# Layer-1 mixer: an earlier start of the k chain, and 16x16 blocks inverted on GpSimd instead of three levels on TensorE

## The chip, the cores and the metric

The kernel runs on 1 core of one Trainium2 chip. The time is device microseconds of that core, as the median of several executions. TensorE is called PE here, VectorE DVE, ScalarE ACT, GpSimd POOL and SyncE SP, as in the profile.

## What is computed

The reference is a two-layer decoder trunk over 256 tokens of width 1024. Each layer is a mixer, a cross-attention into 256 memory tokens and a gated MLP, each followed by `x <- LayerNorm(alpha * x + sublayer(x))`. The change lies in the mixer of layer 1, a chunked gated DeltaNet with 8 heads of 128 and chunks of 64 tokens. Cut to what matters:

```
q, k, v, z, bl, al = split(x @ w_in)            # 4 x 1024 columns, and 2 x 8
q, k, v = split(silu(causal_dwconv(qkv, conv_w)))
qh, kh = l2norm(q) * 128**-0.5, l2norm(k)
beta = sigmoid(bl);  g = -exp(a_log) * softplus(al + dt_bias);  gc = cumsum(g) within a chunk
decay = exp(gc_t - gc_s) for s <= t, else 0
m = strictly lower part of ((kh * beta) kh^T * decay)     # 64x64 for each head and chunk
tinv = inverse of (eye + m)                              # unit lower triangular
u = tinv @ (v * beta);  w = tinv @ (kh * beta * exp(gc))
qk = (qh kh^T) * decay
for each chunk:  v_new = u - w @ state
                 out = (qh * exp(gc)) @ state + qk @ v_new
                 state = state * exp(gc_last) + (kh * exp(gc_last - gc))^T v_new
o = rms_norm(out) * silu(z);  return o @ w_out
```

## The kernel before

Weights come from DRAM in 1 MB pieces on SP's queue (`load`), are split into a rounded part `wh` (ACT, L151) and a rest `wl` (DVE, L153), and each product is made of three PE passes (`mm3`, L158 to L160, and `mm3n`, L164 to L166). One 128-column piece of a projection is 24 such matmuls, and its result goes through the causal convolution (ACT L926, three DVE taps L929) and a Silu (L934).

The 8 heads are worked in two groups of four, and the tokens in two halves `tt` of 128, that is two chunks each. For a group and a half, `gdn_pre` makes the decay `dT` (from `pg`, PE), k, q and v transposed (`pk`, `pq`, `pv`), the products `pK` and `pQ`, the masked and scaled triangle `LT` and its transpose `L` (from `pL`). The inverse `Z` of (eye + m) is then built by doubling: level 0 is a mask and a difference on DVE, and levels 1 to 6 in `gdn_inv` each take two products on PE (`pA` of Z and a part of L, `pZ` of X and A) and one transpose (`pX`), with copies on ACT (`Lc`, `X`, half of the next Z) and a mask and a difference on DVE. `gdn_rec` runs the recursion over the two halves and normalises the result: `pvn`, `pS` and `pon` on PE, `vn` and `zg` on DVE, and a power on POOL (`rsqrt`, L135) between two DVE steps on `zg` (L1131 and L1135).

The order of PE's instructions is written by hand. `weave` runs a chain, a generator whose `yield n` asks for n steps of another generator, the fill, in between; the numbers come from the table `NW`. A fill step is 6 matmuls of a projection, or 3 of 512 columns. Instructions issued before the first `yield 0`, and those of all other engines, are placed by the scheduler of the framework. Every engine runs its own instructions strictly in order.

Before, the gate projection z of group 0, the k projection, `scalars()` (beta and the decay rates g, through `pl` and `pgc`), and the q and v projections of group 0 stand ahead of the chain. The fill of group 0's chain are the k, q and v projections of group 1 (`group_1`), that of group 1's prologue the z projection, and that of the last recursion the output projection (`res["head"]`).

Of the kernel before, what the change touches and what calls it, by code (L numbers as in the profile page):

```python
# [14 lines left out]
ALU = mybir.AluOpType  # L15
# [11 lines left out]
RMS_EPS = 1e-6  # L27
LAM_INIT = 0.8 - 0.6 * math.exp(-0.3 * 0)
NLEV = 6
NTAIL = 8  # L30
NEARLY = 6
AHEAD = 2
NW = [3, 2.6, 1, 2.5, 1, 1.2, 0.7, 3, 2, 3, 4, 1, 6, 2, 0, 5.2, 0.3, 3]
NEG = -1e30

def _constants():
    s = np.arange(P)[:, None]
    t = np.arange(P)[None, :]
# [50 lines left out]
def hybrid_trunk(ctx: ExitStack, tc: tile.TileContext, a: dict, const: dict, out: bass.AP, dbg=None):  # L89
# [110 lines left out]
    def proj_t(*args):  # L200
        run(proj_t_gen(*args))
# [666 lines left out]
    def mixer_c(h, hT, sm, smq, fill, res):  # L868
# [101 lines left out]
        def bank(name):  # L970
            return mm(name).rearrange("p (g t) -> p g t", t=P)
# [16 lines left out]
        tts = nc.vector.tensor_tensor  # L988

        def level_tile():  # L990
            return smq.tile([P, 4, 64], F32, tag="A", name="A")

        def heads(x):
            return x.unsqueeze(1).broadcast_to([x.shape[0], 4, 64])
# [3 lines left out]
            for g in range(4):  # L998
                nc.scalar.activation(junk[:, g], src[:, g], AF.Square, accum_out=dst[:, g:g + 1])

        def gdn_pre(grp, tt, o):
            tsl = slice(tt * P, tt * P + P)
            cs = slice(tt * 8 + grp * 4, tt * 8 + grp * 4 + 4)
            q, k, v = (qkvT[x, grp][:, :, tsl] for x in "qkv")
            sc = sm.tile([P, 6, 4], F32, tag="sc", name="sc", bufs=4)
# [21 lines left out]
            yield NW[7 + grp]  # L1027
            pq = bank("pq")
            tr4(pq, q)
            sum_sq(sc[:, 1], pq)  # L1030
            pv = bank("pv")
            tr4(pv, v)

            nc.vector.tensor_scalar(sc[:, 0:2], sc[:, 0:2], RMS_EPS, None, op0=ALU.add)
# [3 lines left out]
            nc.vector.tensor_scalar(sc[:, 4], sc[:, 1], RMS_EPS * P, None, op0=ALU.mult)  # L1040
            o["b"], o["eq"] = sc[:, 3], sc[:, 4]
            vx = o["vx"] = keep("vx", grp, tt)
            for g in range(4):
                nc.scalar.mul(vx[:, g], pv[:, g], sc[:, 2, g:g + 1])
            if tt:
                tts(qg, qg, q, op=ALU.mult)
            yield
# [11 lines left out]
            pL = bank("pL")
            tr4(pL, LT)  # L1060
            L = o["L"] = t2("L")
            nc.scalar.copy(L, pL)

            Z = o["Z"] = t2("Z")
            nc.scalar.copy(Z, row(C("ident1")))
            A = level_tile()
            zu = Z.rearrange("p g (u r b) -> p g u r b", u=2, r=2)[:, :, :, 1]
            tts(A, LT.rearrange("p g (n u) -> p g n u", u=2)[..., 1], heads(C("imask")), op=ALU.mult)
            tts(zu, zu, A.rearrange("p g (b u) -> p g u b", u=2), op=ALU.subtract)
            yield  # L1070

        def gdn_inv(o):
            Z, L = o["Z"], o["L"]
            for lev in range(1, NLEV + 1):

                last = lev == NLEV
                half = slice(0, 64)
# [32 lines left out]
                yield NW[9] if "kgx" in o and lev == NLEV else None  # L1110
# [339 lines left out]
```

## Time and profile before

| | |
|---|---|
| median of 3 runs | 943.89 us (941.56 to 945.12) |
| the profiled execution | 942.03 us, span 940.3 us |
| mean granted TensorE clock | 0.992 |
| PE busy | 917.3 us, 98% of the span |
| DVE, ACT, POOL busy | 689.1, 532.6, 36.0 us |
| the stretch of the change | about 503 to 659 us of the span |

The times below are us from the start of the span. In a row of a timeline stand the start, how long, the engine, the line, the operation, the tile written and the tiles read, the shape, the number of instructions merged, and in brackets idle time before it and what ended it. Matmuls overlap, so that the distance of two starts says more than a duration. A 32-bit matmul of the chain shows as two instructions.

### The profile page before, as it was taken

To read this page: it belongs to the slowest core of one execution; us is meant where nothing else is said; L and a number is where in the kernel's file an instruction comes from. 1 tells how busy PE (TensorE), PEld (TensorE's weight loads), DVE (VectorE), ACT (ScalarE), POOL (GpSimd) and SP (SyncE) were. 2 spreads that over 40 slices of the span, in tenths; PEclk is the share of its full clock that TensorE was granted. 3 is DMA by queue.
4 is the path that set the end of the run, shared out by engine and by line. 5 is a ranking of instruction groups with operands and counts; after the bars stand their busy time and mean duration, and the time that the engine had idled before them with its cause. 6 is when DMAs were issued, how large, how long until landed. Compare 5 with 4: busy or idle time off the path is not lost. (4 is left out here: it accounts for less than half of the span.)

```text
span 940.3 us, 15842 instructions
## 1 busy us (share of the span) xinstructions
PE 917.3 (98%) x6284; PEld 820.6 (87%) x6284; DVE 689.1 (73%) x1155; ACT 532.6 (57%) x945; POOL 36.0 (4%) x49
## 2 busy tenths in 40 slices
PE   6999999999999999999999999999999999999996
PEld 5887798889988999998889999888889789999885
DVE  5497586776458999984687975754697889999554
ACT  4753466445444766663357876664364476666440
POOL 1000001000000000000010100000200000000000
PEclk9999999999999999999999999997999999999998
DMA  7843345555573566655566441211444546665541
GB/s 247 293 147 108 117 135 183 177 180 179 190 251 97 180 198 209 209 193 182 179 189 190 136 127 54 91 46 45 151 163 136 177 137 213 207 206 182 189 170 45
DMA packets 101715, 152.89 MB, mean 163 GB/s; under 512 B 5225, under 2 KB 73673, under 8 KB 101641
## 3 DMA queue, kind: packets, MB, share of 16 engines
q1 hardware_dynamic: 99576, 145.08, 46.9%
q0 software_dynamic: 2064, 6.80, 2.2%
q8 instruction: 50, 0.82, 0.4%
q14 instruction: 25, 0.20, 0.1%
HBM read 150.81 MB, written 1.05 MB: 162 GB/s over the span
## 5 line engine op out<-in xcount | busy, mean ns | idle before, releaser
L153 DVE TENSOR_TENSOR wl<-raw,wh 128x1024 fp32r<-128x1024 f32 x268 | 325.4, 1222 | 116.0 <-ACT wh L151 113.3
L151 ACT CAST wh<-raw 128x1024 fp32r<-128x1024 f32 x268 | 278.9, 1052 | 229.3 <-PE ps_f L159 53.1
L158 PE MATMUL ps_f<-hT,wh 128*128 128x256 f32 x576 | 159.0, 276 | 0.0
L159 PE MATMUL ps_f<-hT,wh 128*128 128x256 f32 x576 | 159.0, 276 | 0.0
L160 PE MATMUL ps_f<-hT,wl 128*128 128x256 f32 x576 | 159.0, 276 | 0.0
L158 PEld LDWEIGHTS ps_f<-hT,wh 128*128 128x128 f32 x576 | 108.1, 188 | 0.0
L159 PEld LDWEIGHTS ps_f<-hT,wh 128*128 128x128 f32 x576 | 108.1, 188 | 0.0
L160 PEld LDWEIGHTS ps_f<-hT,wl 128*128 128x128 f32 x576 | 108.1, 188 | 0.0
L158 PE MATMUL ps_t<-hT,wh 128*128 128x256 f32 x352 | 100.5, 286 | 0.0
L159 PE MATMUL ps_t<-hT,wh 128*128 128x256 f32 x352 | 97.9, 278 | 0.0
L160 PE MATMUL ps_t<-hT,wl 128*128 128x256 f32 x352 | 97.8, 278 | 0.0
L164 PE MATMUL ps_o<-wh,aT 128*128 128x512 f32 x176 | 69.2, 393 | 0.0
L165 PE MATMUL ps_o<-wl,aT 128*128 128x512 f32 x176 | 68.8, 391 | 0.0
L166 PE MATMUL ps_o<-wh,aT 128*128 128x512 f32 x176 | 68.6, 390 | 0.0
L158 PEld LDWEIGHTS ps_t<-hT,wh 128*128 128x128 f32 x352 | 66.1, 188 | 0.7
L159 PEld LDWEIGHTS ps_t<-hT,wh 128*128 128x128 f32 x352 | 66.4, 189 | 0.1
L160 PEld LDWEIGHTS ps_t<-hT,wl 128*128 128x128 f32 x352 | 66.3, 188 | 0.0
L302 PE MATMUL ps<-wh,hT 128*128 128x512 f32 x192 | 54.3, 401 | 0.0
L302 PEld LDWEIGHTS ps<-wh,hT 128*128 128x128 f32 x192 | 36.0, 191 | 8.4 <-DVE hT L381 0.5
L1311 ACT ACTIVATE fy<-ps_f,fcw 128x256 f32<-128x256 f32 x72 | 40.2, 559 | 0.0
L164 PEld LDWEIGHTS ps_o<-wh,aT 128*128 128x128 f32 x176 | 33.0, 188 | 7.6 <-issue 0.5
L166 PEld LDWEIGHTS ps_o<-wh,aT 128*128 128x128 f32 x176 | 33.0, 188 | 7.3
(359 smaller groups left out, 1843.0 us busy)
## 6 DMA issues: line engine op xcount, KB each, us to landing
raw<-in_ffn_w_in SPq DMA_DIRECT2D x44, 1024.0 KB, 5.5
raw<-in_w_in SPq DMA_DIRECT2D x26, 1024.0 KB, 5.7
raw<-in_ffn_w_out SPq DMA_DIRECT2D x22, 1024.0 KB, 5.0
raw<-in_xa_wkv SPq DMA_DIRECT2D x16, 1024.0 KB, 5.3
raw<-in_w_mix_out SPq DMA_DIRECT2D x8, 1024.0 KB, 5.1
raw<-in_xa_wq SPq DMA_DIRECT2D x8, 1024.0 KB, 7.9
raw<-in_xa_wo SPq DMA_DIRECT2D x8, 1024.0 KB, 5.0
lngb<-in_ln_g POOLq DMA_DIRECT2D x6, 512.0 KB, 4.5
```

The source lines that it names most:

```text
L151: nc.scalar.copy(hi, src)
L153: nc.vector.tensor_tensor(lo, src, hi.bitcast(F32), op=ALU.subtract)
L158: nc.tensor.matmul(ps, lh, rh, start=first, stop=False)
L159: nc.tensor.matmul(ps, lh, rl, start=False, stop=False)
L160: nc.tensor.matmul(ps, ll, rh, start=False, stop=last)
L164: nc.tensor.matmul(ps, lh, rh, start=first, stop=False)
L165: nc.tensor.matmul(ps, lh, rl, start=False, stop=False)
L166: nc.tensor.matmul(ps, ll, rh, start=False, stop=last)
L302: nc.tensor.matmul(ps, x, ww[:, k], start=k0 + k == 0 and ww is wh and not xl, stop=k0 + k == KT - 1 and ww is wl)
L1311: nc.scalar.activation(yt, ps, AF.Identity, scale=cw[:, 2, mc:mc + 1], bias=cw[:, 3, mc:mc + 1])
```

## The change

- Levels 1 to 3 go, and level 0 with them. `LT` is written to DRAM (L1048), read back as 64 blocks of 16x16, one to a partition (`base_load`, L1086), and each block's inverse is found by substitution on POOL (`base_solve`: one scaling, 14 times a product and a difference, one memset). The result goes to DRAM (L1100) and comes back (`zc`, L1104) to be spread into `Z` by two DVE products (L1113). `gdn_inv` then does levels 4 to 6.
- `gdn_pre` is cut in two: `gdn_pre_k` needs k alone and ends with `L`; `gdn_pre_q` does q, v and `pQ`.
- The chain starts when k is there. The projections q and v of group 0, then k, q, v of group 1, then z, are one line of fill; `until` gives fill until a named projection is made. After group 0's solve is issued come q and v, then `gdn_pre_q`, k of group 1, `gdn_inv`; after group 1's solve come the recursion of group 0, v, `gdn_pre_q` and `gdn_inv` of group 1.

```diff
-NW = [3, 2.6, 1, 2.5, 1, 1.2, 0.7, 3, 2, 3, 4, 1, 6, 2, 0, 5.2, 0.3, 3]
+NW = [3, 2.6, 1, 2, 1, 1.5, 0.7, 1, 1, 8, 4, 1, 6, 2, 0, 5.2, 0.5, 2]
...
-        def gdn_pre(grp, tt, o):
+        def gdn_pre_k(grp, tt, o):
...
+            nc.gpsimd.dma_start(scr_in[grp][tt * 4:tt * 4 + 4, :P * P].rearrange("g (s t) -> s g t", t=P), LT)
+            pL = bank("pL")
+            tr4(pL, LT)
+            L = o["L"] = t2("L")
+            nc.scalar.copy(L, pL)
+            yield
...
+        def base_load(grp):
+            src = scr_in[grp].rearrange("a b -> (a b)").rearrange("(p x) -> p x", x=BASE * (P + 1))
+            src = src[:, :BASE * P].rearrange("p (i t) -> p i t", t=P)[:, :, :BASE]
...
+            nc.gpsimd.dma_start(m, src)
...
+        def base_solve(grp, os_):
+            m, z = blocks[grp]
+            eng = nc.gpsimd
+            eng.tensor_scalar(z, m, -1.0, None, op0=ALU.mult)
+            for i in range(1, BASE - 1):
...
+                eng.tensor_tensor(t, z[:, :i, i:i + 1].broadcast_to(sh), m[:, i:i + 1, i + 1:].broadcast_to(sh), op=ALU.mult)
+                eng.tensor_tensor(z[:, :i, i + 1:], z[:, :i, i + 1:], t, op=ALU.subtract)
+            eng.memset(z.rearrange("p i j -> p (i j)")[:, ::BASE + 1], 1.0)
+            nc.gpsimd.dma_start(scr_out[grp], z.rearrange("p i j -> p (i j)"))
...
+                nc.gpsimd.dma_start(zc, back[tt])
...
-            for lev in range(1, NLEV + 1):
+            for lev in range(4, NLEV + 1):
...
-        proj_t(*proj_c(0, "q"))
-        proj_t(*proj_c(0, "v"))
...
-        fill.gens.append(group_1())
-        yield from steps(NW[3], gdn_pre(0, 0, os_[0][0]), gdn_pre(0, 1, os_[0][1]))
-        yield from steps(NW[4], gdn_inv(os_[0][0]), gdn_inv(os_[0][1]))
-        fill.rest()
-        fill.gens.append(proj_z(1))
-        yield from steps(NW[5], gdn_pre(1, 0, os_[1][0]), gdn_pre(1, 1, os_[1][1]))
+        fill.gens += [fills(), proj_z(1)]
+        yield from units(NW[3], gdn_pre_k, 0)
+        base_load(0)
+        base_solve(0, os_[0])
+        yield from until("v", 0)
+        yield from units(NW[7], gdn_pre_q, 0)
+        yield from until("k", 1)
+        yield from inv(NW[4], 0)
+        yield from until("q", 1)
+        yield from units(NW[5], gdn_pre_k, 1)
+        base_load(1)
+        base_solve(1, os_[1])
         outs = []
-        yield from steps(NW[16], gdn_inv(os_[1][0]), gdn_inv(os_[1][1]), gdn_rec(0, os_[0], outs))
-        fill.rest()
+        yield from steps(NW[8], gdn_rec(0, os_[0], outs))
+        yield from until("v", 1)
+        yield from units(NW[8], gdn_pre_q, 1)
+        yield NW[9]
...
+        yield from inv(NW[16], 1)
```

First place: PE behind the k projection. `pl` transposes the scalars, `pgc` sums the decay rates, `ps_t` is a projection. Before:

```order
L160 MATMUL ps_t_5179<-hT_4502,wl_5116 128x256
L899 MATMUL pl_5209<-c_all_96,linT_5044 128x16 x4
L158 MATMUL ps_t_5252<-hT_4501,wh_5238 128x256
L159 MATMUL ps_t_5252<-hT_4503,wh_5238 128x256
L160 MATMUL ps_t_5252<-hT_4501,wl_5239 128x256
```

Now:

```order
L160 MATMUL ps_t_5185<-hT_4502,wl_5122 128x256
L899 MATMUL pl_5215<-c_all_96,linT_5050 128x16 x4
L917 MATMUL pgc_5232<-gg_4964,c_m1_4955 128x16 x2
L990 MATMUL pg_5244<-c_m1_4955,gg_4964 128x128 x4
L986 MATMUL pk_5249<-c_all_96,ck_5074 128x128 x4
L990 MATMUL pg_5268<-c_m1_4955,gg_4964 128x128 x4
L986 MATMUL pk_5273<-c_all_96,ck_5074 128x128 x4
L158 MATMUL ps_t_5308<-hT_4501,wh_5294 128x256
```

49 fill matmuls stood between `pl` and `pgc` before, and 143 more ahead of the first `pg`; now none does.

Second place: POOL around the norms of group 0's recursion (`sc_6444`, `sc_6489` now; `sc_6694`, `sc_6771` before). Before:

```order
L1037 TENSOR_TENSOR sc<-sc,phalf 128x4 x4
L135 TENSOR_TENSOR sc_6694<-sc_6694,mhalf 128x4
L135 TENSOR_TENSOR sc_6771<-sc_6771,mhalf 128x4
L135 TENSOR_TENSOR sc_7048<-sc_7048,mhalf 128x4
L393 DMA lngb<-in_ln_g 128x1024
L135 TENSOR_TENSOR sc_7103<-sc_7103,mhalf 128x4
```

Now, with the end of group 1's solve:

```order
L1098 TENSOR_TENSOR base<-base,bt 64x11x4
L1097 TENSOR_TENSOR bt<-base 64x36
L135 TENSOR_TENSOR sc_6444<-sc_6444,mhalf 128x4
L1098 TENSOR_TENSOR base<-base,bt 64x12x3
L1097 TENSOR_TENSOR bt<-base 64x26
L1098 TENSOR_TENSOR base<-base,bt 64x13x2
L1097 TENSOR_TENSOR bt<-base 64x14
L1098 TENSOR_TENSOR base<-base,bt 64x14
L1100 DMA scr_out<-base 64x256
L1104 DMA zc<-scr_out 128x4x16 x2
L135 TENSOR_TENSOR sc_6489<-sc_6489,mhalf 128x4
```

The first norm's power stands behind 25 of the solve's 30 instructions, and the second behind all of it, the store of the result and the issue of its two loads.

Third place: DVE in the recursion of group 0, between the two values `vn`. Before:

```order
L1131 TENSOR_TENSOR zg<-pon,h 128x512
L1133 SCALAR_TENSOR_TENSOR sc_6694<-sc_6694,sc 128x4
L1089 TENSOR_TENSOR A<-pA,c_m_4955 64x256
L1135 TENSOR_TENSOR zg<-zg,sc_6694 128x512
L1124 TENSOR_TENSOR vn<-pvn,sc 128x512
L1108 TENSOR_TENSOR Z<-Z,pZ 128x8x32 x2
L1131 TENSOR_TENSOR zg<-pon,h 128x512
L1133 SCALAR_TENSOR_TENSOR sc_6771<-sc_6771,sc 128x4
```

Now:

```order
L1166 TENSOR_TENSOR vn<-pvn,sc 128x512
L1173 TENSOR_TENSOR zg<-pon,h 128x512
L1175 SCALAR_TENSOR_TENSOR sc_6444<-sc_6444,sc 128x4
L929 SCALAR_TENSOR_TENSOR cv<-ps_t,gcw,cv 128x253
L1177 TENSOR_TENSOR zg<-zg,sc_6444 128x512
L929 SCALAR_TENSOR_TENSOR cv<-ps_t,gcw,cv 128x254
L1166 TENSOR_TENSOR vn<-pvn,sc 128x512
L929 SCALAR_TENSOR_TENSOR cv<-ps_t,gcw,cv 128x255
L153 TENSOR_TENSOR wl<-raw,wh 128x1024
L1173 TENSOR_TENSOR zg<-pon,h 128x512
```

The multiplication of `zg` by the power (L1177, before L1135) still stands ahead of the second `vn`; behind it now stand taps of the convolution and weight splits instead of the steps of the levels.

## Rows read from the trace of the kernel before

**Rows 1.** The page, busy time of each engine, share of the span, instructions.

```profile
PE 917.3 (98%) x6284; PEld 820.6 (87%) x6284; DVE 689.1 (73%) x1155; ACT 532.6 (57%) x945; POOL 36.0 (4%) x49
```

**Rows 2.** Timeline of PE in the mixer, the rows after a wait of its own.

```profile
541.29 1.16 PE L986 MATMUL pK<-ck 128*128 128x128 f32 x8 [1.20 <-ACT vx L1044]
...
603.60 0.66 PE L982 MATMUL pq<-c_all,cq 128*128 128x128 f32 x4 [1.04 <-ACT kq L1019]
...
615.47 0.68 PE L986 MATMUL pA<-Z,Lc 128*64 128x64 f32 x8 [0.75 <-ACT Lc L1081]
...
636.39 1.97 PE L986 MATMUL pZ<-A,X 64*128 64x64 f32 x16 [0.59 <-ACT Z L1101]
```

**Rows 3.** Windows: length, busy of PE, PEld, DVE, ACT, POOL, granted clock, DMA, GB/s.

```profile
648.40:658.80 10.40, 9.84 (x61) 9.19 (x60) 3.54 (x7) 2.70 (x5) 0.00 (x0) 0.52 0.16 61
```

**Rows 4.** Timeline of PE, one level of group 0 (start us, us, instruction, count).

```profile
551.10 0.68 PE L986 MATMUL pA<-Z,Lc 128*64 128x64 f32 x8
...
552.88 0.63 PE L1092 MATMUL pX<-c_all,Z 128*64 128x128 f32 x4
553.26 0.37 PE L158 MATMUL ps_t<-hT,wh 128*128 128x256 f32 x1
...
554.60 0.28 PE L160 MATMUL ps_t<-hT,wl 128*128 128x256 f32 x1
554.81 2.00 PE L986 MATMUL pZ<-A,X 64*128 64x64 f32 x16
556.73 0.38 PE L158 MATMUL ps_t<-hT,wh 128*128 128x256 f32 x1
```

**Rows 5.** Timelines of PE and ACT, from the scalars to the first Silu of k.

```profile
501.99 1.06 PE L899 MATMUL pl<-c_all,linT 32*128 32x16 f32 x8
...
505.91 1.05 ACT L151 CAST wh<-raw 128x1024 fp32r<-128x1024 f32 x1 [0.66 <-PE ps_t L159]
506.98 1.28 ACT L907 ACT_TABLE_LOAD   x1
...
509.01 0.59 PE L917 MATMUL pgc<-gg,c_m 128*128 128x16 f32 x4 [0.19 <-issue]
...
509.88 1.28 ACT L920 ACT_TABLE_LOAD   x1
...
511.38 1.28 ACT L934 ACT_TABLE_LOAD   x1
512.67 1.34 ACT L934 ACTIVATE ck<-cv 128x256 f32<-128x256 f32 x4
```

**Rows 6.** Groups by line of DVE: a weight split, and one convolution tap.

```profile
L153 DVE TENSOR_TENSOR wl<-raw,wh 128x1024 fp32r<-128x1024 f32 x268 | 325.4, 1222 | 116.0 <-ACT wh L151 113.3 <-PE pl L899 0.2
...
L929 DVE SCALAR_TENSOR_TENSOR cv<-ps_t,gcw,cv 128x253 f32<-128x253 f32 x24 | 11.3, 475 | 6.6 <-ACT cv L926 6.4
```

**Rows 7.** Timeline of PE, after the first wait of the program.

```profile
10.28 1.97 PE L377 MATMUL pt<-c_all,h 128*128 128x128 f32 x8 [3.67 <-DMA h<-in_x]
11.90 2.31 PE L302 MATMUL ps<-wh,hT 128*128 128x512 f32 x6
...
14.52 1.54 PE L302 MATMUL ps<-wh,hT 128*128 128x512 f32 x6
```

**Rows 8.** Groups by line of POOL: count, busy us, mean ns, idle before.

```profile
L135 POOL TENSOR_TENSOR sc<-sc,mhalf 128x4 f32<-128x4 f32 x4 | 4.1, 1014 | 58.1 <-DVE sc L1133 53.8 <-ACT wh L151 4.4
L1037 POOL TENSOR_TENSOR sc<-sc,phalf 128x4 f32<-128x4 f32 x4 | 4.9, 1228 | 122.5 <-DVE sc L1036 122.5
L1435 POOL MEMSET const-float32-1.0<- 128x1 f32 x1 | 0.1, 100 | 0.0
```

**Rows 9.** DMA issues: count, KB each, median us from issue to landing.

```profile
out<-h SPq DMA_DIRECT2D x4, 256.0 KB, 2.0
...
raw<-in_w_in SPq DMA_DIRECT2D x2, 64.0 KB, 6.1
...
ng<-in_gdn_norm POOLq DMA_DIRECT2D x1, 0.5 KB, 2.3
```

More of the change, by code (lines that the diff above doesn't have):

```diff
@@ L29 @@
 NLEV = 6
+BASE = 16
 NTAIL = 8
@@ L64, in _constants @@
     add("m1", "sums", np.concatenate([s <= t, s > t], axis=1))
-    add("m1", "imask", masks[0][:, halves[0]])
-    add("m1", "cmasks", np.concatenate([s % (64 >> lev) == t[:, :64] % (64 >> lev) for lev in range(1, NLEV)], axis=1))
-    add("m1", "ident1", s == t // 64 * 2 + t % 32 * 4 + t % 64 // 32)
+    add("m1", "blocks", s[:, :1] // BASE == np.arange(P // BASE)[None, :] % 4 * 2 + np.arange(P // BASE)[None, :] // 4)
+    add("m1", "cmasks", np.concatenate([s % (64 >> lev) == t[:, :64] % (64 >> lev) for lev in range(4, NLEV)], axis=1))
     add("m1", "dmask", np.where(s <= t, 0.0, NEG))
@@ L958, in t2 @@
             return smq.tile(B4, F32, tag="t2", name=name, bufs=8)
+        scr = ctx.enter_context(tc.tile_pool(name="scr", bufs=2, space=bass.MemoryType.DRAM))
+        scr_in = [scr.tile([8, P * (P + 1)], F32, name="scr_in") for _ in range(2)]
+        scr_out = [scr.tile([8 * P // BASE, BASE * BASE], F32, name="scr_out") for _ in range(2)]
         held = {}
@@ L990, in level_tile @@
         def level_tile():
-            return smq.tile([P, 4, 64], F32, tag="A", name="A")
+            return smq.tile([P, 4, 64], F32, tag="A", name="A", bufs=2)
         def heads(x):
@@ L999, in sum_sq @@
                 nc.scalar.activation(junk[:, g], src[:, g], AF.Square, accum_out=dst[:, g:g + 1])
-        def gdn_pre(grp, tt, o):
+        def gdn_pre_k(grp, tt, o):
             tsl = slice(tt * P, tt * P + P)
             cs = slice(tt * 8 + grp * 4, tt * 8 + grp * 4 + 4)
-            q, k, v = (qkvT[x, grp][:, :, tsl] for x in "qkv")
-            sc = sm.tile([P, 6, 4], F32, tag="sc", name="sc", bufs=4)
+            k = qkvT["k", grp][:, :, tsl]
+            sc = o["sc"] = sm.tile([P, 6, 4], F32, tag="sc", name="sc", bufs=4)
             pg = bank("pg")
@@ L1026, in gdn_pre @@
                 tts(kg, pk, col(egs[:, 1, cs]), op=ALU.mult)
[L1027 to L1036, printed above, removed]
+            yield
+            nc.vector.tensor_scalar(sc[:, 0], sc[:, 0], RMS_EPS, None, op0=ALU.add)
             nc.gpsimd.tensor_tensor(sc[:, 2], sc[:, 0], phalf, op=ALU.pow)
@@ L1039, in gdn_pre @@
             nc.vector.tensor_tensor(sc[:, 3], sc[:, 3], beta[:, tt, grp * 4:grp * 4 + 4], op=ALU.mult)
-            nc.vector.tensor_scalar(sc[:, 4], sc[:, 1], RMS_EPS * P, None, op0=ALU.mult)
             o["b"], o["eq"] = sc[:, 3], sc[:, 4]
[L1042 to L1047, printed above, removed]
             pK = bank("pK")
@@ L1053, in gdn_pre, with gdn_pre_q @@
                                                op0=ALU.mult, op1=ALU.mult)
+            yield
+            nc.gpsimd.dma_start(scr_in[grp][tt * 4:tt * 4 + 4, :P * P].rearrange("g (s t) -> s g t", t=P), LT)
[3 more added lines that the diff above has]
+            nc.scalar.copy(L, pL)
+            yield
+        def gdn_pre_q(grp, tt, o):
+            tsl = slice(tt * P, tt * P + P)
+            q, k, v = (qkvT[x, grp][:, :, tsl] for x in "qkv")
+            sc, dT = o["sc"], o["att"]
+            pq = bank("pq")
+            tr4(pq, q)
+            sum_sq(sc[:, 1], pq)
+            pv = bank("pv")
+            tr4(pv, v)
+            nc.vector.tensor_scalar(sc[:, 4], sc[:, 1], RMS_EPS, RMS_EPS * P, op0=ALU.add, op1=ALU.mult)
+            vx = o["vx"] = keep("vx", grp, tt)
+            for g in range(4):
+                nc.scalar.mul(vx[:, g], pv[:, g], sc[:, 2, g:g + 1])
+            if tt:
+                tts(o["qg"], o["qg"], q, op=ALU.mult)
+            yield
             pQ = bank("pQ")
@@ L1057, in gdn_pre @@
             yield
[L1059 to L1062, printed above, removed]
-            Z = o["Z"] = t2("Z")
[L1065 to L1069, printed above, removed]
@@ L1070, in gdn_pre @@
-            yield
-        def gdn_inv(o):
-            Z, L = o["Z"], o["L"]
-            for lev in range(1, NLEV + 1):
+        nb = 8 * P // BASE
+        blocks = {}
+        def base_load(grp):
+            src = scr_in[grp].rearrange("a b -> (a b)").rearrange("(p x) -> p x", x=BASE * (P + 1))
+            src = src[:, :BASE * P].rearrange("p (i t) -> p i t", t=P)[:, :, :BASE]
+            m, z = lnp.tile([P, 512], F32, tag="tok", name="base")[:nb].rearrange("p (a i j) -> a p i j", a=2, j=BASE)
+            nc.gpsimd.dma_start(m, src)
+            blocks[grp] = m, z
@@ new lines, in base_solve @@
+        def base_solve(grp, os_):
[3 more added lines that the diff above has]
+            for i in range(1, BASE - 1):
+                sh = [nb, i, BASE - 1 - i]
+                t = sm.tile([nb, 64], F32, tag="bt", name="bt")[:, :sh[1] * sh[2]].rearrange("p (i j) -> p i j", i=i)
+                eng.tensor_tensor(t, z[:, :i, i:i + 1].broadcast_to(sh), m[:, i:i + 1, i + 1:].broadcast_to(sh), op=ALU.mult)
+                eng.tensor_tensor(z[:, :i, i + 1:], z[:, :i, i + 1:], t, op=ALU.subtract)
+            eng.memset(z.rearrange("p i j -> p (i j)")[:, ::BASE + 1], 1.0)
+            nc.gpsimd.dma_start(scr_out[grp], z.rearrange("p i j -> p (i j)"))
+            back = scr_out[grp].rearrange("(t g b) (i j) -> t (b i) g j", t=2, g=4, j=BASE)
+            for tt in range(2):
+                zc = os_[tt]["zc"] = sm.tile([P, 4, BASE], F32, tag="zc", name="zc")
+                nc.gpsimd.dma_start(zc, back[tt])
@@ L1076, in gdn_inv @@
+        def gdn_inv(o):
+            zc, L = o["zc"], o["L"]
+            Z = o["Z"] = t2("Z")
+            for u in range(2):
+                sh = [P, 4, BASE, 4]
+                tts(Z[:, :, 64 * u:64 * u + 64].rearrange("p g (r b) -> p g r b", b=4),
+                    zc.unsqueeze(3).broadcast_to(sh),
+                    C("blocks")[:, 4 * u:4 * u + 4].unsqueeze(1).unsqueeze(1).broadcast_to(sh), op=ALU.mult)
+            for lev in range(4, NLEV + 1):
                 last = lev == NLEV
@@ L1088, in gdn_inv @@
                 else:
-                    tts(A, pA, heads(cmasks[half, lev - 1]), op=ALU.mult)
+                    tts(A, pA, heads(cmasks[half, lev - 4]), op=ALU.mult)
                 pX = bank("pX")[half, :, cols]
@@ L1109, in gdn_inv @@
                     Z = o["Z"] = Z2
-                yield NW[9] if "kgx" in o and lev == NLEV else None
+                yield
             if "kgx" in o:
@@ L1184, in mixer_c, with fills, until, units @@
             finish()
-        proj_t(*proj_c(0, "q"))
-        proj_t(*proj_c(0, "v"))
-        def group_1():
-            for nm in "kqv":
-                yield from proj_t_gen(*proj_c(1, nm))
-        yield 0
-        fill.gens.append(group_1())
-        yield from steps(NW[3], gdn_pre(0, 0, os_[0][0]), gdn_pre(0, 1, os_[0][1]))
-        yield from steps(NW[4], gdn_inv(os_[0][0]), gdn_inv(os_[0][1]))
-        fill.rest()
-        fill.gens.append(proj_z(1))
-        yield from steps(NW[5], gdn_pre(1, 0, os_[1][0]), gdn_pre(1, 1, os_[1][1]))
+        made = set()
+        def fills():
+            for grp in range(2):
+                for nm in "kqv"[1 - grp:]:
+                    yield from proj_t_gen(*proj_c(grp, nm))
+                    made.add((nm, grp))
+        def until(nm, grp):
+            while (nm, grp) not in made:
+                yield 1
+        def units(n, gen, grp, *args):
+            return steps(n, *(gen(grp, tt, os_[grp][tt]) for tt in range(2)))
+        def inv(n, grp):
+            return steps(n, *(gdn_inv(os_[grp][tt]) for tt in range(2)))
+        yield 0
+        fill.gens += [fills(), proj_z(1)]
[10 more added lines that the diff above has]
+        base_solve(1, os_[1])
         outs = []
-        yield from steps(NW[16], gdn_inv(os_[1][0]), gdn_inv(os_[1][1]), gdn_rec(0, os_[0], outs))
-        fill.rest()
+        yield from steps(NW[8], gdn_rec(0, os_[0], outs))
+        yield from until("v", 1)
+        yield from units(NW[8], gdn_pre_q, 1)
+        yield NW[9]
         new = new_t("oT")
```

## The prediction

> **What bounds the kernel now.** I read the page's busy line first, then the timeline of TensorE (PE) through the layer-1 mixer, then the windows of that stretch, then the rows that price what is new. PE is busy 98% of the span [rows 1], and the mixer holds no long gap: between 503 and 659 us I find single waits of 0.59 to 1.20 us [rows 2]. So whatever PE stops doing shortens the kernel, and whatever makes PE wait lengthens it, microsecond for microsecond. VectorE, ScalarE and GpSimd count only where PE ends up waiting for them. Beside the waits there is one slow stretch: from 648.4 to 658.8 us the granted clock is 0.52 [rows 3], which is the 1.2 GHz level of 1.2 and 2.4, after some 17 us of small matmuls with little fill between.
>
> **The change, part by part.** All is summed against the profiled execution, 942.03 us (span 940.3); the median of the three runs, 943.89, lies 1.9 above it.
>
> *Three levels leave PE.* One level for both token halves is pA, pX, pA, pX, from 551.10 to 553.26, and two pZ, from 554.81 to 556.73 [rows 4]: 2.16 + 1.92 = 4.08 us. Three levels in two groups are 6 x 4.08 = 24.5 us. Each cut between fill and chain also costs about 0.1 us (the last of twelve fill matmuls starts at 554.60, one pitch is 0.12, pZ starts at 554.81 [rows 4]); six cuts fewer net, with the extra pieces of the split prologue, are 0.8. Together **-25.3 us**. VectorE and ScalarE lose their shares of the levels too; PE hid them, so that is worth nothing.
>
> *Old waits go.* The four waits [rows 2] sum to 3.6 us and the places they stand at are rearranged: **-3.6**. The slow clock ran in group 1's levels with almost no fill. That section is now half as long and has one line of fill in it, so I take the 10.4 x 0.48, less the 0.56 us of wait inside it, as gone: **-4.5**.
>
> *The chain begins too early for its scalars.* Before, 49 fill matmuls stand between pl and pgc, and 143 between pgc and pg; now pl, pgc, pg, pk follow each other (the first of the three places of the written order). What PE waits for is in [rows 5]. pl ends at 503.05; the exponent on ScalarE ends at 505.25 (0.66 before the cast at 505.91). Without that cast a table load of 1.28 starts there, and from the end of that load to pgc it took 0.75 (508.26 to 509.01): pgc starts at 507.3, and PE waits 4.2 us. From the end of pgc there are ngc, a table load (1.28), egs, a table load (1.28) and the first Silu, 3.4 us, of which pg hides 0.9; the four Silus (1.34 together) then pace pk by another 0.6. That is 4.2 + 2.5 + 0.6 = **+7.3 us**. No other work covers it: PE runs in its written order and the k projection has ended.
>
> *Smaller new waits.* The second LT now comes behind ScalarE's squares, a table load and a VectorE cast; by the size of the same pair's waits before (1.20 and 1.04 [rows 2]) I take 2 us at pL. pv now stands straight behind the last matmuls of v, whose tile still needs three taps of 0.475 [rows 6], a scaling and a Silu: 1.5. Group 1's recursion loses a piece of fill: 1.5. Together **+5**.
>
> *Restart of the clock.* After 3.67 us of idle at the start of the program six 512-column matmuls took 2.31 us and soon after six took 1.54 [rows 7]. A wait of 5 to 8 us should cost 1 to 2 us in that way: **+1.9** for the first.
>
> *The new side chain.* LT goes to DRAM, comes back as 16x16 blocks, is solved by 30 GpSimd instructions that each wait for the one before, and goes out and in once more. No row shows a plain product or difference on GpSimd. Below stands the memset, 0.10 us; above stand the powers on the same kind of tile, 1.01 and 1.23 us [rows 8]. By form the new instructions are nearest to the power, by work to the memset, with some 14 to 56 columns instead of 1; I take 0.3, three memsets, and keep 0.1 to 1.23 for the range. For the transfers I have a 256 KB store of 2.0 us, a 64-byte-row load of 64 KB with 6.1 us, and 2.3 for the smallest [rows 9]: I take 3 for LT out, 5 for the blocks in, 2.8 for the result out, 3.5 for it back. The whole is 3 + 5 + 30 x 0.3 + 2.8 + 3.5 = 23.3 us from the second LT (from 12 to 55 at the ends).
>
> Group 0: VectorE meets Z<-zc where PE has done pL, 150 fill matmuls (18 us at the pitch of 0.12) and pq, and the last tap has come: about 21 us. It stops for some 2.3; two weight pieces already split (48 matmuls, 5.8 us) less VectorE's own backlog give PE about 4 us. So nothing reaches PE: **0**, up to 34.
>
> Group 1 is worse, and the order shows why (second and third place). The rsqrt of the recursion's first norm stands in GpSimd's queue behind 25 of the 30 instructions, and VectorE, which runs in order, stops at zg until it is there; vn, the taps and the weight splits queue behind zg. Counted from the end of pK: LT 3.6, transfers 8, 25 x 0.3, rsqrt 1.0, then zg, a tap and vn 1.9, so PE could go on at 22, and without the queue it would be there at 15: **+7**. The second rsqrt stands behind the last five, the store's landing and two issues: 1.5 + 2.9 + 1.2 + 1.0, then VectorE's zg, split, taps and the Silu, 3.7, against PE at pv 6.3 after the first: **+4**. One more restart: **+1.9**.
>
> **Sum:** 942.0 - 25.3 - 3.6 - 4.5 + 7.3 + 5 + 1.9 + 0 + 7 + 4 + 1.9 = **935.7** for an execution like the profiled one, 0.7% faster. Against the median I would say 1.9 more, and I settle between: 937. Without any GpSimd wait it is 922.8; each 0.1 us on one GpSimd instruction adds 3 us (25 and 5 in group 1), and 6 once group 0 stops hiding, from about 0.36.
>
> A page speaks against this step. In rows, a weight split on VectorE takes 1.22 us [rows 6] and reads two SBUF tiles; three of them fall into each solve. The Trainium skill, "SBUF — State Buffer", section "Who interferes with whom", says that a VectorE instruction with two SBUF inputs and a GpSimd instruction that reads SBUF exclude each other for the whole instruction. No row here shows the two together. The Trainium skill, "GPSIMD Engine Reference", section "3.1 Elementwise — side-by-side cycle accounting", gives 2.6 cycles an element and a 1.2 GHz engine; by it 56 elements are 0.12 us, and with little else in an instruction the sum would be near 931, an estimate.
>
> **The rivals.**
>
> *All hidden.* With transfers at their shortest and instructions of 0.1 us group 1's rsqrt comes before PE wants it: 923. For it: the memset row. Against it: no row of a reading instruction on GpSimd is below 1 us.
>
> *Shared port.* Three splits of 1.22 lengthen the solve by 3.7 us in group 0, of which 2 reach PE, and about 2.4 in group 1: 936 + 5 = 941. For it: splits are the most common VectorE work [rows 6]; against it: VectorE itself stands still for much of group 1's solve. This is the mechanism of the first page named above.
>
> *GpSimd too slow.* The mechanism of the sum with one other number. At 0.7 us an instruction group 0 costs 9 us and a restart, group 1 17 and 6: 922.8 + 32 + 4 = 959, slower by 1.6%. It decides from about 0.43 us, where the total is back at 942. For it: the powers at 1.01 and 1.23 [rows 8]; against it: their arithmetic.
>
> That the change does not do what it says is excluded: the written order shows the levels gone and the chain begun.
>
> **How the numbers follow.** A measurement of this kernel tells about 0.5% from no change, 4.7 us. Forecast 0.43, mostly 928 to 940; all hidden 0.13; shared port 0.16; too slow 0.28. Faster: 0.13 + nine tenths of 0.43, 0.52. Same: the port case, the edge of the forecast and a little of the slow one, 0.22. Slower: 0.26. The range from 921 to 959 leaves out a tenth at each end.
>
> **What would show it.** Right: twelve fewer pairs of pA and pX rows and no clock of 0.5 between the last levels; PE idle 4 to 5 us before pgc and 2 to 4 before pk, ended by ScalarE; VectorE idle at L1177 ended by GpSimd; L1097 and L1098 near 0.3 us from start to start. Wrong: a pitch above 0.45 there, VectorE waiting more than 5 us at the first L1113 for zc, or PE not waiting at pgc at all.

## Result and profile after: 1.2% slower

The changed kernel takes 953.93 us (median of 4, 953.29 to 954.76) against 942.95 for the kernel before in the same comparison: ratio 1.0115, 95% interval 1.0091 to 1.0139. The forecast was 937 us, faster than before. The profiled execution has a span of 952.7 us, 12.4 more than before.

These are the busy line of the page of the changed kernel, called after here (to be held beside [rows 1]), and the span and mean granted clock of its core:

```profile
PE 903.3 (95%) x6044; PEld 806.0 (85%) x6044; DVE 681.6 (72%) x1131; ACT 518.6 (54%) x907; POOL 66.4 (7%) x121
core 0: 952.7 us, clock 0.976
```

PE is busy 14.0 us less, yet idle 26.4 us more (49.4 against 23.0): together the 12.4. The mean clock fell from 0.992 to 0.976. Both losses lie in the mixer. These are PE's timeline rows there that have idle time before them, in brackets with what ended it; three rows of 0.53 to 0.88 us at the end of the mixer and one of 0.47 are left out:

```profile
506.00 1.00 PE L917 MATMUL pgc<-gg,c_m 128*128 128x16 f32 x4 [4.25 <-issue]
510.51 1.39 PE L986 MATMUL pk<-c_all,ck 128*128 128x128 f32 x4 [1.61 <-ACT ck L934]
...
541.41 0.33 PE L986 MATMUL pv<-c_all,cv 128*128 128x128 f32 x1 [0.53 <-ACT cv L934]
544.05 0.33 PE L986 MATMUL pv<-c_all,cv 128*128 128x128 f32 x1 [2.31 <-ACT cv L934]
...
565.02 0.73 PE L990 MATMUL pA<-Z,Lc 128*64 128x64 f32 x8 [4.31 <-DVE Z L1113]
...
621.56 2.08 PE L990 MATMUL pon<-vn,dT 128*128 128x128 f32 x8 [11.05 <-DVE vn L1166]
...
631.50 0.33 PE L986 MATMUL pv<-c_all,cv 128*128 128x128 f32 x1 [2.76 <-ACT cv L934]
...
646.88 0.67 PE L990 MATMUL pA<-Z,Lc 128*64 128x64 f32 x8 [2.08 <-DVE Z L1113]
```

All waits of the mixer sum to 31.4 us, where before had 4.3 by the same rows (some of them in [rows 2]). Of the seven waits of more than 1 us six are followed by a stretch at the 1.2 GHz level (clock 0.50, or between 0.5 and 1 where a window is slow in part); the exception is the 2.76 us at pv. Windows of after (length, busy PE, PEld, DVE, ACT, POOL, granted clock, DMA, GB/s), to be held against [rows 3]:

```profile
505.00:510.00 5.00, 2.90 (x12) 2.63 (x12) 1.34 (x6) 3.40 (x6) 0.00 (x0) 0.50 0.56 190
510.00:515.00 5.00, 4.49 (x23) 4.12 (x24) 1.26 (x5) 4.41 (x16) 0.00 (x0) 0.57 0.00 0
545.00:550.00 5.00, 5.00 (x33) 5.00 (x32) 0.00 (x0) 2.67 (x15) 2.76 (x6) 0.66 0.49 152
565.00:570.00 5.00, 4.98 (x32) 4.65 (x33) 0.42 (x1) 1.46 (x4) 0.00 (x0) 0.66 0.46 174
620.00:625.00 5.00, 3.44 (x16) 3.44 (x17) 3.18 (x6) 1.56 (x9) 2.76 (x7) 0.50 0.07 15
650.00:655.00 5.00, 5.00 (x20) 4.13 (x21) 1.44 (x3) 1.30 (x3) 0.00 (x0) 0.50 0.00 0
```

What the clock costs I estimate as busy time of PE times one minus the granted clock, over windows of 1 us: 14.5 us in the mixer of after (3.3 at 506 to 515, 1.7 at 545, 1.7 at 565, 2.7 at 621, 5.1 at 647 to 658), 4.8 before. One check on the estimate: the work from the last wait for Z to the first pz takes 30.6 us here and 26.1 in e9 below, where the clock stays at 1.00, so that 4.5 us stand against the 5.1. So the sum is 27.1 us more waits, 9.7 more slow clock, and 23.7 less work (14.0 + 9.7); that makes 13.1, 0.7 more than the 12.4 of the spans; the 0.7 lie in the rest of the program.

The side chain, first GpSimd's own rows in group 0:

```profile
531.18 0.87 POOL L1093 TENSOR_SCALAR base<-base 64x256 f32<-64x256 f32 x1 [4.09 <-DMA base<-scr_in]
532.13 0.20 POOL L1097 TENSOR_TENSOR bt<-base 64x14 f32<-64x14 f32 x1
...
532.42 0.20 POOL L1098 TENSOR_TENSOR base<-base,bt 64x14 f32<-64x14 f32 x1
532.70 1.12 POOL L1097 TENSOR_TENSOR bt<-base 64x26 f32<-64x26 f32 x1
533.90 0.23 POOL L1098 TENSOR_TENSOR base<-base,bt 64x26 f32<-64x26 f32 x1
...
535.58 1.31 POOL L1098 TENSOR_TENSOR base<-base,bt 64x44 f32<-64x44 f32 x1
536.97 0.28 POOL L1097 TENSOR_TENSOR bt<-base 64x50 f32<-64x50 f32 x1
...
546.02 0.62 POOL L1100 DMA_DIRECT2D scr_out<-base  x1 [0.29 <-POOL base L1098]
548.31 1.57 POOL L1104 DMA_DIRECT2D zc<-scr_out  x2 [1.67 <-DMA scr_out<-base]
```

and VectorE's in the same time:

```profile
532.52 1.22 DVE L153 TENSOR_TENSOR wl<-raw,wh 128x1024 fp32r<-128x1024 f32 x1
...
535.55 1.22 DVE L153 TENSOR_TENSOR wl<-raw,wh 128x1024 fp32r<-128x1024 f32 x1
536.68 1.51 DVE L929 SCALAR_TENSOR_TENSOR cv<-ps_t,gcw,cv 128x253 f32<-128x253 f32 x3
...
551.87 0.76 DVE L1113 TENSOR_TENSOR Z<-zc,c_m 128x256 f32<-128x256 f32 x2 [8.39 <-DMA zc<-scr_out]
```

A plain GpSimd instruction takes 0.20 to 0.30 us and follows the one before at 0.3 to 0.36. Five of group 0's take 0.63 to 1.38 instead: each overlaps a VectorE product or difference of two SBUF tiles and ends 0.1 us after it (533.82 against 533.74 for the first, 532.70 + 1.12 and 532.52 + 1.22). Beside the taps, which read PSUM, it is 0.28. The five lose 4.3 us, and the solve takes 14.6 us, 0.49 an instruction. From the second LT (522.8) to zc (551.9) it is 29 us, and VectorE stands for 8.39.

Group 1, GpSimd and then VectorE:

```profile
618.50 0.24 POOL L1097 TENSOR_TENSOR bt<-base 64x36 f32<-64x36 f32 x1
618.70 1.03 POOL L135 TENSOR_TENSOR sc<-sc,mhalf 128x4 f32<-128x4 f32 x1
619.72 0.25 POOL L1098 TENSOR_TENSOR base<-base,bt 64x36 f32<-64x36 f32 x1
```

```profile
619.77 0.75 DVE L1177 TENSOR_TENSOR zg<-zg,sc 128x512 f32<-128x512 f32 x1 [10.08 <-POOL sc L135]
620.44 0.47 DVE L929 SCALAR_TENSOR_TENSOR cv<-ps_t,gcw,cv 128x254 f32<-128x254 f32 x1
620.83 0.67 DVE L1166 TENSOR_TENSOR vn<-pvn,sc 128x512 f32<-128x512 f32 x1
```

The rsqrt runs between two instructions of the solve, zg waits 10.08 us for it, vn stands behind zg, and PE's last pon of group 0 waits 11.05 for vn.

### The profile page after: what moved, and what is told of

It is laid out like the page before. It is cut to its first block, busy times and chain, and to the rows that moved or that the text cites. A ratio compares the mean times of both kernels' runs of the same rounds, so it can differ in the third digit from the quotient of the medians.

```text
span 952.7 us, 15344 instructions
## 1 busy us (share of the span) xinstructions
PE 903.3 (95%) x6044; PEld 806.0 (85%) x6044; DVE 681.6 (72%) x1131; ACT 518.6 (54%) x907; POOL 66.4 (7%) x121
## 5 line engine op out<-in xcount | busy, mean ns | idle before, releaser
L158 PE MATMUL ps_t<-hT,wh 128*128 128x256 f32 x352 | 102.7, 292 | 0.0
L159 PE MATMUL ps_t<-hT,wh 128*128 128x256 f32 x352 | 99.5, 283 | 0.0
L158 PEld LDWEIGHTS ps_t<-hT,wh 128*128 128x128 f32 x352 | 68.5, 194 | 0.5
L159 PEld LDWEIGHTS ps_t<-hT,wh 128*128 128x128 f32 x352 | 68.4, 194 | 0.1
L135 POOL TENSOR_TENSOR lnmv<-lnmv,mhalf 128x1 f32<-128x1 f32 x12 | 11.4, 947 | 479.3 <-DVE lnmv L408 479.3
L164 PEld LDWEIGHTS ps_o<-wh,aT 128*128 128x128 f32 x176 | 33.0, 188 | 7.6 <-issue 0.5
```

The source lines that it names most:

```text
L135: nc.gpsimd.tensor_tensor(dst, src, mhalf[:, :n], op=ALU.pow)
L158: nc.tensor.matmul(ps, lh, rh, start=first, stop=False)
L159: nc.tensor.matmul(ps, lh, rl, start=False, stop=False)
L164: nc.tensor.matmul(ps, lh, rh, start=first, stop=False)
```

## The experiments

Two theories. *Cover*: the levels are worth their 25 us, but the new order leaves too little work between a producer and PE in several places, VectorE's in-order queue carries each delay to PE, and PE pays twice, idle and at 1.2 GHz. *Price*: the solve on GpSimd costs what it saves, wherever it stands. Ratios are to the kernel before in the same comparison, and gains below go by the difference of ratios (0.1% is 0.94 us) unless medians are named.

| run | median us | ratio | interval |
|---|---|---|---|
| change | 953.93 | 1.0115 | 1.0091 to 1.0139 |
| e1 | 946.07 | 1.0036 | 1.0013 to 1.0060 |
| e2 | 946.26 | 1.0054 | 1.0035 to 1.0073 |
| e3 | 950.68 | 1.0105 | 1.0071 to 1.0139 |
| e4 | 962.58 | 1.0209 | 1.0179 to 1.0239 |
| e5 | 955.27 | 1.0157 | 1.0135 to 1.0179 |
| e6 | 958.07 | 1.0187 | 1.0156 to 1.0217 |
| e7 | 938.78 | 0.9981 | 0.9963 to 0.9999 |
| e8 | 939.57 | 1.0000 | 0.9978 to 1.0022 |
| e9 | 945.32 | 1.0038 | 1.0019 to 1.0057 |
| e10 | 946.93 | 1.0052 | 1.0033 to 1.0071 |
| e11 | 919.28 | 0.9761 | 0.9738 to 0.9783 |
| e12 | 959.60 | 1.0186 | 1.0163 to 1.0210 |

**e1, the rsqrt off GpSimd's queue.**

```diff
-                rsqrt(sc[:, 2], sc[:, 1], 4)
+                if grp:
+                    rsqrt(sc[:, 2], sc[:, 1], 4)
+                else:
+                    nc.scalar.activation(sc[:, 2], sc[:, 1], AF.Sqrt)
+                    nc.vector.reciprocal(sc[:, 2], sc[:, 2])
```

> The changed kernel, but the rsqrt of group 0's recursion is a square root on ScalarE and a reciprocal on VectorE, so that it no longer stands in GpSimd's queue behind the solve of group 1. Queue theory (that place in the queue is the cause in group 1): the 11.05 us wait of PE before pon falls under 2 us, and the slow clock after it goes as well, 938 to 941 us. Latency theory (the transfers and the solve together are longer than the work that covers them): VectorE comes to the first Z<-zc of group 1 some 8 to 12 us before zc has landed and stops there in its place, PE waits 6 to 8 us a little later, and the time is 946 to 951 us.

The 11.05 us wait is gone and 7.4 us are won. The median lies at the lower edge of the latency theory's range, well above the queue theory's, and VectorE's rows in e1 show that theory's mark, the stop again one step later:

```profile
633.09 0.76 DVE L1113 TENSOR_TENSOR Z<-zc,c_m 128x256 f32<-128x256 f32 x2 [8.95 <-DMA zc<-scr_out]
```

PE then waits 5.04 us at pv, a little less than expected. The queue was a cause, and the late zc behind it the next one.

**e2, no solve steps.**

```diff
-            for i in range(1, BASE - 1):
+            for i in range(1, 1):
```

> The changed kernel without the 28 product and difference instructions of each solve (the inverse that comes out is not the reference's); the scaling, the memset and all transfers stay. If GpSimd's instructions are what makes the side chain too long: zc of group 0 lands some 13 us earlier, VectorE's 8.4 us stop at the first Z<-zc and PE's 4.3 us wait go, the 11 us wait goes, and the time is 934 to 941 us. If the transfers are what makes it too long (some 14 us in each group), the waits stay at more than half their length and the time is 946 us or more. The waits of PE before pgc and pk (4.25 and 1.6 us) stay in both.

By the number it is the second branch, by the rows neither: VectorE no longer stops in group 0, so the transfers aren't too long there, but of PE's 4.31 us 2.69 stay. In group 1 the rsqrt, which now stood behind the zc issues, still came late, since the load of the blocks alone took 7.8 us from its issue: 7.54 us at zg, 10.6 us of waits at pv. Even without solve steps the change is 0.5% slower than before. So the price of GpSimd's instructions alone is not the cause.

**e3, PE kept busy in two waits.**

```diff
+            if not grp:
+                spin(90)
             mm4(pon, lambda g: o1["att"][:, g], lambda g: vn[:, g], start=False)
...
+            spin(34)
             pg = mm("pgc")
```

> The changed kernel with useless matmuls of fill size in two of PE's waits, 34 before pgc and 90 before the last pon of group 0; nothing reads their result. The waits themselves are as long as before, only PE is not idle in them. Clock theory (each wait is paid a second time, because PE comes out of it at 1.2 GHz): the granted clock is 1.0 from 621 to 630 us and higher from 506 to 515, and the time is 948 to 951 us. Rival (the slow clock belongs to the chain's small 32-bit matmuls, not to the waits): clock and time stay as they are, 953 to 955 us.

The 90 matmuls fill 610.49 to 621.45, and the window behind them, as well as the one behind pgc, now reads 1.00:

```profile
505.00:510.00 5.00, 2.54 (x21) 2.18 (x19) 1.48 (x6) 3.80 (x8) 0.00 (x0) 1.00 0.55 184
...
620.00:625.00 5.00, 5.00 (x43) 4.83 (x42) 1.63 (x3) 2.08 (x10) 2.45 (x4) 1.00 0.15 26
```

That is the clock theory's mark. The median, 950.68, lies in its range too, but that the time moved is not shown: six executions lie between 948.15 and 958.12, and the interval takes in the change's own ratio. The run is also harder on PE than I meant it to be. VectorE had finished vn at 619.35 (the load of the blocks took 4.2 us, not 6.3), so that the 90 matmuls held PE 1.9 us too long, and pk then waits 2.51 us for 1.61, pv 3.43 for 2.76.

**e4, the order alone, levels back on PE.**

```diff
-            for lev in range(4, NLEV + 1):
+            Z, L = o["Z"], o["L"]
+            for lev in range(1, NLEV + 1):
...
-        base_load(0)
-        base_solve(0, os_[0])
```

(with level 0 and its constants as before, and the same for group 1.)

> The changed kernel's order of work (chain begun after k, one line of fill) with the inverse as it was before: levels 0 to 3 on VectorE and TensorE, no scratch transfers, no solve on GpSimd. It shows what the order alone does. If the early start is harmful by itself (waits of 5.9 us before pgc and pk, 2 to 3 at pv, and the slow clock behind them): 949 to 957 us, slower than the kernel before. If the order is harmless and all loss is the side chain's: 941 to 945 us. The waits for vn and for Z in group 0 and the slow clock behind these should be gone in both.

More than either: 19.7 us slower than before, 16.4 us of waits and 10.0 of slow clock in the mixer. It isn't the order in a pure form, since six levels use more of the fill and leave its end bare. But it says which part is harmful: against e4 the change is 9 us faster, so the solve, with all its stalls, is the part that gains.

**e5, the start covered.**

```diff
+        yield 6
         run(extra)
         for finish in late:
             finish()
...
+        yield 4
         yield from units(NW[3], gdn_pre_k, 0)
```

(for this the fill is set up earlier, and Silus of the fill are held back together with k's.)

> The changed kernel with 6 fill steps (36 matmuls, 4.3 us) taken between pl and pgc and 4 (2.8 us) between pgc and the first pg; the Silus of k follow pgc as before. Start theory (the chain begins before its scalars are there, and PE pays for it twice, idle and at 1.2 GHz): the waits of 4.25 and 1.6 us and the slow clock from 506 to 515 us go, some 9 us. Trade theory (these 60 matmuls are missing afterwards as cover of group 0's solve): VectorE's stop at the first Z<-zc grows from 8.4 to some 15 us, PE's wait for Z from 4.3 to 9 to 11 us, and the whole is 950 to 954 us, no gain. If the two don't hang together: 943 to 946 us.

As the trade theory has it, at a smaller size: the start falls from 5.86 to 1.66 us, PE's wait for Z grows to 6.30 with 1.24 more at a fill matmul before it, VectorE's stop grows to 11.88 where I had 15, and pL waits 2.28. Nothing is won; at 955.27 it is even a little worse than I said.

**e6, the same on e4.**

```diff
+        yield 6
         run(extra)
...
+        yield 4
         yield from units(NW[3], gdn_pre_k, 0)
```

> The order of work alone (run e4: inverse on TensorE as before, 962.6 us, 19.7 above the kernel before by the ratio) with the same 6 and 4 fill steps at the start. No solve here needs cover. If the start is the larger part of what the order costs: 950 to 955 us, 8 to 12 less than e4. If the order costs elsewhere (pv right behind v, pL, the norms of group 1 at the end): 957 us or more.

2.1 us less than e4 by the ratios, 4.5 by the medians, with intervals that overlap. As far as four executions of each tell, the start is a smaller part of the order's cost than its own rows say; by e6's rows the rest is pv, pL and the late levels.

**e7, both solves early.**

```diff
+            for nm, grp in (("k", 1), ("q", 0), ("v", 0), ("q", 1), ("v", 1)):
...
+        yield from until("k", 1)
+        yield 2
+        yield from units(1, gdn_pre_k, 1)
+        base_load(1)
+        base_solve(1, os_[1])
         yield from until("v", 0)
```

(with e5's start, one fill step instead of 2 and 1.5 between the pieces of the two `gdn_pre_k`, another pool for group 1's L, four buffers for `zc`, and the same lines taken out further down.)

> Fill in the order k1, q0, v0, q1, v1, z1, so that the k part of both groups comes first and both solves run on GpSimd while q and v of group 0 and group 0's inverse are on TensorE; the start covered by 6 and 4 fill steps; group 1's L in another pool. Latency theory (the levels are worth 25 us, and the side chain of some 29 us only has to be covered by the work that is there): no stop of VectorE at the first Z<-zc, no wait for the rsqrt, slow clock only in group 1's last levels: 917 to 926 us, faster than both kernels. Rival (the solve on GpSimd costs what it saves wherever it stands, through the shared port and the queues): 936 us or more.

My 917 to 926 was wrong; 938.78 lies in the rival's range, but not for its reason: VectorE no longer stops at the first Z<-zc and PE's wait behind the rsqrt is gone, but 22 us of short waits are left (pL 6.4, pv 5.5, pA 4.8 among them).

**e8, e7 with longer solves.**

```diff
-                eng.tensor_tensor(t, z[:, :i, i:i + 1].broadcast_to(sh), m[:, i:i + 1, i + 1:].broadcast_to(sh), op=ALU.mult)
+                for _ in range(2):
+                    eng.tensor_tensor(t, z[:, :i, i:i + 1].broadcast_to(sh), m[:, i:i + 1, i + 1:].broadcast_to(sh), op=ALU.mult)
```

> Run e7 with every product instruction of the solves issued twice, 14 more instructions of 0.2 to 0.3 us in each group, some 5 us each. If the solves are hidden in e7: within 3 us of e7. If GpSimd sets the time: 5 to 10 us more.

0.8 us more by the medians (1.8 by the ratios, with intervals that overlap) for 14 more instructions in each group. By GpSimd's rows the two solves, up to the issue of the store, take 18.3 and 16.8 us where e7 had 11.6 and 12.4, and VectorE still stops at no Z<-zc. The solves are hidden there, and the price theory falls.

**e9, Z of both halves at once.**

```diff
         def inv(n, grp):
+            for tt in range(2):
+                gdn_base(os_[grp][tt])
```

(`gdn_base` is the part of `gdn_inv` with the two products.)

> The changed kernel, but the products that spread zc into Z are issued for both token halves before the first level, so that on VectorE the second half's no longer stand behind taps and weight splits of the fill. If PE's wait for the second Z is VectorE's order of work (2.69 us of it remained in e2, with no solve steps): the waits of 4.31 us in group 0 and 2.08 us in group 1 fall to under 2 and 0.5 us, and 946 to 950 us; 943 if the slow clock behind the second goes too. If it is the late zc alone: no change, 952 to 955 us.

7.3 us won. VectorE still stops for 8.84 us at the first of these products, yet of PE's two waits for Z, 4.31 us has become 1.06 (at pZ) and 2.08 has become 0.34, and there is no slow clock behind either:

```profile
554.22 1.43 DVE L1111 TENSOR_TENSOR Z<-zc,c_m 128x256 f32<-128x256 f32 x4 [8.84 <-DMA zc<-scr_out]
```

```profile
566.60 1.97 PE L990 MATMUL pZ<-A,X 64*128 64x64 f32 x16 [1.06 <-DVE A L1132]
```

In the change the second half's product stood behind taps and a split, as VectorE's rows there show:

```profile
560.07 1.51 DVE L929 SCALAR_TENSOR_TENSOR cv<-ps_t,gcw,cv 128x253 f32<-128x253 f32 x3
561.50 1.21 DVE L153 TENSOR_TENSOR wl<-raw,wh 128x1024 fp32r<-128x1024 f32 x1
...
564.47 0.41 DVE L1113 TENSOR_TENSOR Z<-zc,c_m 128x256 f32<-128x256 f32 x1
```

**e10, fill before pv.**

```diff
         yield from until("v", 0)
+        yield 4
```

(and the same for group 1.)

> The changed kernel with 4 fill steps (24 matmuls, 2.8 us) between the last matmuls of a v projection and pq and pv, in both groups; they are taken from the steps that follow anyway. The waits before pv (0.53 and 2.31 us in group 0 with 1.7 us of slow clock behind, 2.76 us in group 1) go: 946 to 950 us. If VectorE's stop at Z<-zc then only comes out as a longer wait for Z: 951 to 955 us.

5.9 us won, at the lower end of the first expectation. Of the waits at pv 0.25 us stay. Z waits 1.4 us longer, so part was passed on. The last pon of group 0 waits 1.4 longer too, but the edit need not be the cause: the load of group 1's blocks took 7.6 us there, 1.4 more than in the change.

**e11, everything covered.** e7 with the edits of e9 and e10, and

```diff
-        yield 6
+        yield 9
...
-        yield from units(1, gdn_pre_k, 0)
+        yield from units(2, gdn_pre_k, 0)
...
-        yield from units(1, gdn_pre_k, 1)
+        yield from units(2, gdn_pre_k, 1)
```

> Run e7 (both solves early, 938.8 us) with its remaining waits covered by fill steps taken earlier: 9 before pgc, 2 in place of 1 per piece in the k part of both groups, 4 before pq and pv, and the products into Z of both halves at once. e7 had 22 us of PE waits and 6.3 us of slow clock in the mixer. If these short waits are what is left of the change's cost: 918 to 928 us, faster than both kernels. If covering one only opens the next (the fill is used up by the last levels): 932 to 939 us.

919.28 us, 2.4% faster than the kernel before, as expected. Its span is 918.6 us, its mean clock 0.994, and its busy line:

```profile
PE 893.3 (97%) x6044; PEld 798.1 (87%) x6044; DVE 680.9 (74%) x1131; ACT 516.8 (56%) x907; POOL 66.3 (7%) x121
```

The waits of the mixer are 8.2 us and its slow clock 3.2. Which of these edits gave how much was not separated.

**e12, that order with the levels on PE.** e11 with e4's edit in the inverse, and

```diff
-        yield from inv(NW[4], 0)
+        yield from inv(0.5 * NW[4], 0)
...
-        yield from inv(NW[16], 1)
+        yield from inv(0.5 * NW[16], 1)
```

> The order of work and the fill of run e11 (919.3 us), with the inverse as it was before: levels 0 to 3 on VectorE and TensorE, no scratch transfers, no solve; half as much fill for each of the twice as many steps of the levels. If the solve on GpSimd is worth its three levels (25.3 us) once it is covered: 942 to 950 us. If e11 gains by its order instead and the solve adds little: 920 to 935 us.

40 us slower than e11, far over the 942 to 950 of the first theory: PE is busy 33.4 us longer (926.7), 6.5 of it slow clock, and waits 6.3 longer, of which 4.91 are one wait at the transposes (pt) behind the mixer's LayerNorm. So the order alone gains nothing here either; with these fill steps it pays only together with the solve.

## Why the prediction was wrong

The sum, term by term; the measured value is wait plus slow clock behind it, in the profiled execution.

| term | predicted | measured |
|---|---|---|
| levels, cuts | -25.3 | -23.7 |
| old waits | -3.6 | -4.3 |
| start of the chain, restart | +9.2 | +9.2 |
| pL | +2 | 0 |
| pv of group 0 | +1.5 | +4.5 |
| recursion | +1.5 | +0.5 |
| group 0's solve | 0 | +6.0 |
| group 1, first rsqrt, restart | +8.9 | +13.7 |
| group 1, second rsqrt (PE at pv) | +4 | +2.8 |
| last levels: old slow clock gone | -4.5 | +2.4 |
| norms and LayerNorm at the end | 0 | +2.0 |

- **Right:** the mechanism of group 1, the place of the start and its first wait (4.25 us against 4.2), the transfers of group 0 (3.4, 4.9, 2.3, 3.5 against 3, 5, 2.8, 3.5), VectorE's arrival at the first Z<-zc (21 us after the second LT). **Luck:** that the start sums to 9.2 in both columns; pk waited 1.61 us for 3.1, and the slow clock cost 3.3 for 1.9. The measured time lies inside 921 to 959 by luck too: the upper end stood for slow GpSimd instructions.
- **First failed step:** "The slow clock ran in group 1's levels with almost no fill. [...] so I take [it] as gone." It came back: within 1 us of the end of PE's 2.08 us wait for the second Z the clock is at the 1.2 GHz level, and it stays there for 10 us. With that wait gone, e9 shows no such stretch. 6.9 us off; how long the stretch lasts is not settled by the wait, since behind the same wait e2 and e3 lose only 1.6 and 1.5 us.
- **Second:** "So nothing reaches PE: 0". The solve took 14.6 us where the sum had 9: 1.3 of it is the pitch, 4.3 the port. VectorE stopped 8.4 us instead of 2.3; a wait of more than 5 us there was one of my signs of being wrong. The 4.31 us at PE look like that stop less my 4 us of cover, but that is a coincidence: PE's fill runs without a gap to 559.5, long after the stop, e2 and e7 show waits of 2.69 without any such stop, and e9 leaves 1.06 with a stop of 8.84. The wait hung on VectorE's order: I had costed the first half's product and never asked where the second half's stands. 6.0 us off.
- **Third:** the wait behind the rsqrt, 11.05 for 7: from the last LT to the issue of the base load it took 3.9 us where I had 3, the load 6.3 where I had 5, and 25 instructions 8.6 where I had 7.5. The load's share shows in the four traces that have this wait: loads of 4.2, 6.3, 7.6 and 7.8 us (e5, after, e10, e9) go with waits of 8.91, 11.05, 12.41 and 12.59. Slow clock 2.7 for 1.9. 4.8 us off.
- **Fourth:** pv, where three taps, scaling and Silu cost 2.8 us instead of 1.5 and a slow stretch that I had not counted. 3 us off.

Read against e4 instead of the rows, the order is the larger miss. The terms that belong to the order alone (old waits, old slow clock, start, smaller waits) come to +6.1 us in the sum; e4 took 19.7, though its six levels also use more of the fill. The terms of the solve (levels, group 0, both rsqrts) come to -12.4; from e4 to the change it is -9.

The rival "GpSimd too slow" had the sign, not the price: it took 0.7 us an instruction, and they took 0.49 in group 0 (with the port) and 0.35 in the 25 of group 1, so its 959 is not what happened. An instruction of 56 elements beside which no such VectorE instruction ran took 0.28 to 0.30 us, not the 0.12 of the prediction's estimate near 931. The shared port is real, and in group 0 it costs the solve 4.3 us where I had 3.7; of the wait at PE the whole stop explains at most 1.6 us (4.31 less the 2.69 of e2). The Trainium skill, "SBUF — State Buffer", section "Who interferes with whom", says that the two exclude each other; the trace agrees, with the five long instructions of 0.63 to 1.38 us. And of the restarts of the clock I priced two, at 1.9 each; in after six waits have slow clock behind them.

Open: the clock's share in time (e3's spread), and how e4's 20 us divide between order and fill. Between the profiled executions of e4 and of the kernel before lie 22.0 us: 12.1 are waits, 5.1 slow clock, and the rest is busy time of PE that neither accounts for.

## What to carry to other kernels

Work taken off a full engine is worth its busy time only if every consumer on the way, in the order in which its queue runs, still has something to do: go through each in-order queue and ask of every new wait what stands behind it. A wait of PE often costs a second time in clock, so covering a few short waits can be worth nearly as much as the work that was removed (e7 to e11: 19.5 us by the medians and 16.0 between the profiled executions, for the same matmuls). When a side chain is long, begin all of its instances early, before the fill is used up.

## What the runs showed of the hardware

- A GpSimd product or difference that meets a VectorE product or difference of two SBUF tiles lasts until that ends (0.28 becomes up to 1.38 us); beside a tap, which reads PSUM, it does not (0.28).
- The loss in slow clock behind a wait hardly depends on the wait's length: 1.7 us behind 1.66 us of idle time in e5, 1.9 behind 8.91. Not every wait has it: none is seen behind the waits of up to 1.20 us in [rows 2], nor behind 2.76 us in after, 2.69 in e2 and 3.43 in e3. And the slow clock comes without a wait, too: in e4 it is 0.50 from 674 to 679 us, among the small matmuls of the last levels, and PE had not waited since 628.
- The same wait can be followed by a short or a long slow stretch. In e1 the rows at 565 us stayed slow for 14 us (6.4 lost), in after for 4 (1.7), behind nearly the same wait (4.71 and 4.31). The runs of e1 fall in two clusters, 940.4 to 942.3 us with a mean clock of 0.983 to 0.986 and 946.0 to 949.2 with 0.971 to 0.982, which would fit; that this is the reason was not tested.
- The load of the 64 blocks, the same transfer each time, took between 3.0 us (e11) and 7.8 us (e9) from its issue to the GpSimd instruction that reads it.
